# One more step of distance between scores, transpositions and products with V, in two attention loops of a transformer kernel

## Chip, cores and metric

The kernel runs on one core of a Trainium2 chip. The metric is the device time of one execution in microseconds (us); lower is better. The engines of the core are TensorE (PE in the profile, with PEld for its weight loads), VectorE (DVE), ScalarE (ACT), GpSimd (POOL) and SyncE (SP, which here only issues DMAs). Each engine takes its own instructions strictly in order and waits on semaphores of the others.

## The reference, cut to what matters

The reference is two blocks of two layers each. The first block is sparse attention with a short convolution, then latent attention, each followed by an MLP; the change doesn't touch it. The second block has a layer of differential attention and a layer of neighbourhood attention over 512 latent tokens and 256 context tokens, with 2048 inner features. Cut to its core:

```python
def diff_softmax_pair(q, k, v, lam, scale):          # 16 heads of two score maps each, V of width 128
    s = jnp.einsum('bqnd,bknd->bnqk', q, k) * scale
    p = jax.nn.softmax(s, axis=-1)                   # keys: 512 latent + 256 context
    w = p[:, :, 0] - lam * p[:, :, 1]
    return jnp.einsum('bhqk,bkhe->bqhe', w, v)
# then: rms_norm(o, subln_g) * (1 - lam_init) * silu(z) @ w_out

# neighbourhood attention, 32 heads of width 64, for one row of queries:
    s = einsum(q_row, k_band) * scale + bias          # masked outside the window
    p = softmax(concat([s, s_ctx]))
    o = einsum(p_band, v_band) + einsum(p_ctx, v_ctx)
# then: o * silu(z) @ w_out
```

Both layers begin with the projections q, k, v and z of their normalized input.

## The kernel before

All products are made in a split form: every operand x is kept as a high part and a low part (x minus the high part), and three matmuls stand for one (`mm3`, lines 578 to 580). The weights are split on the way in: `WeightStream.split` copies the high part on ACT (line 272) and subtracts on POOL (line 273). A ring of four split units is kept; `hold` releases the used ones, and each `tick` splits at most one more.

Both attention layers run through `second`. It plans a loop of steps by hand: `fill[i]` holds the "pieces" of step i (24 matmuls of a projection into one 128x256 tile of PSUM, named `mm`, some 2.85 us of PE), `early[i]` and `extra[i]` hold small work for ACT, DVE, POOL and the queues. The pieces of head group g + 1 (q, k, v) and of z of group g are made between the attention steps of group g, so PE always has matmuls to go on with. `defer` puts work off to the beginning of the next step.

**Differential attention** (`diff_run`): 8 groups g, 2 pairs p, 6 query tiles t, so 96 units and 12 steps to a group. The text counts steps inside a group from 0; step 12 is step 0 of the next group. In step i:

- A: scores of unit i into the PSUM tiles `s2` (2 buffers of 1024 columns), for the two maps. Tiles t = 0 to 3 have 768 keys ("wide"), t = 4 and 5 have the 256 context keys.
- B on DVE: the negated row maximum (L2051). E on ACT: the exponentials, with their row sums. `Dm` on DVE: the reciprocal (L2071), two scalings (L2072), the weighted difference (L2073, tile `X`) and EPS times the squared row sum (L2076, tile `oe`).
- T of unit i - 1: PE transposes the difference (L2088) into PSUM tiles `tp` (2 buffers; a wide unit takes two, a narrow one one); ACT and DVE copy it to `wt`.
- G of unit i - 2: the product with V (L2101), 12 matmuls in what the trace counts for a wide unit, 4 for a narrow one.
- `Hn` and `H2` follow a pair's last tile: norm of the output, then six transpositions into two `tp` tiles (L2128), scaled on DVE by z's gate (L2129), and a DMA to DRAM. H2 comes HD = 6 steps after the last tile's scores, at the end of steps 11 (pair 0) and 5 of the next group (pair 1).
- `stack` (L1778), in `extra`: transposes q or k of the next group into one `tp` tile and splits it; at the end of steps 6, 7, 8, 9, 11 (two of them), 12 and 13.

**Neighbourhood attention** (`na_run`): 8 groups, 4 heads, 4 query tiles, so 128 units and 16 steps to a group. A (L2212, L2213) makes 512 scores, B (L2221) adds bias and takes the maximum, E the exponentials, `Dm` reciprocal and scaling (L2231, L2232, tile `X`). T of unit i - 1 is four transpositions (L2239); ACT copies the high part `pth`, DVE makes the low part `ptl`. After the fourth tile of a head, G (L2249, L2254) multiplies with V, and `add` (L2261) on DVE joins the halves one step later. Steps 12 to 17 end with stacks of the next group; `dup` copies the upper half of KH and KL by a DMA on POOL's queue (L1802) after steps 14 and 17, and the scores of step 16 need the first of them. `tp` has 3 buffers here.

The order of a step on PE is A, the first piece (neighbourhood: its first half), T (neighbourhood: G, then T), the remaining pieces, G (differential), H2, stacks.

Of the kernel before, what the change touches and what calls it, by code (L numbers as in the profile page):

```python
# [12 lines left out]
F32 = mybir.dt.float32  # L13
# [215 lines left out]
Z7 = (3, 4, 5, 6, 7, 7)  # L229
Y7 = (7, 7, 7, 7, 8, 8, 8, 8)  # L230
O7 = [9, 10, 10, 11, 11, 12, 12, 13, 14, 15, 16, 17]
Z73 = (2, 2, 3, 4)
Y73 = (4, 4, 5, 5, 5, 6, 6, 6)
O73 = [7 + j for j in range(10)]
O1 = (59, 62, 64, 66)
# [138 lines left out]
class Net:  # L374
# [1240 lines left out]
    def second(s, L, nx):  # L1615
# [222 lines left out]
        for g in range(8):  # L1838
            t0 = ns * g
            zz = [z_piece(g, b, t) for b in range(2) for t in range(0, qw, 256)]  # L1840
            qk = [piece("q", g + 1, i) for i in range(nq)] + [piece("k", g + 1, i) for i in range(6)]
            if diff and g < 7:
                vv = [piece("v", g + 1, i) for i in range(6)]
                rest = zz + vv if g < 6 else zz[:3] + vv + zz[3:]
                for t, x in zip((6, 6, 7, 7, 8, 8, 9, 9, 10, 10, 11, 11) if g < 6 else (6, 7, 8, 8, 9, 10, 11, 12, 13, 13, 14, 15), rest):
                    put(fill, t0 + t, x)
                for j in range(6):
                    put(fill, t0 + j, *qk[2 * j:2 * j + 2])
                at = (6, 6, 7, 8, 8, 9, 9, 10, 11, 12, 13, 14) if g < 6 else (6, 7, 7, 8, 8, 9, 13, 13, 14, 14, 15, 15)
                gates_at([t0 + t for t in at], g, [(b, c) for b in range(2) for c in range(6)])  # L1850
                for t, f in zip((6, 7, 8, 9), stacks("q", 0) + stacks("k", 0)):
                    put(extra, t0 + t, f)
                put(extra, t0 + 9, lambda: dup(0))
                for t, f in zip((11, 11, 12, 13), stacks("q", 1) + stacks("k", 1)):
                    put(extra, t0 + t, f)
                put(extra, t0 + 13, lambda: dup(1))
            elif diff:
                for t, x in zip(Z7, zz):
                    put(fill, t0 + t, x)
                put(extra, t0 + 2, lambda: y_tile(), *[lambda b=b: y_dma(b) for b in range(5)])  # L1860
                gates_at([t0 + t for t in (4, 5, 6, 7, 8, 9, 10, 11, 12, 13, 14, 15)], g, [(b, c) for b in range(2) for c in range(6)])
                put(extra, t0 + 5, lambda: y_dma(5))
                for b in range(8):
                    put(early, t0 + Y7[b], lambda b=b: y_split(b))
            else:
                if g < 7:
                    vv = [piece("v", g + 1, i) for i in range(6)]
                    for t, x in zip((0, 1, 2, 3, 4, 5, 6, 7, 8, 9, 10, 11, 12, 13) + ((13, 14, 14, 15, 15, 16) if g < 6 else (14, 15, 15, 16, 16, 17)), qk + zz + vv):
                        put(fill, t0 + t, x)
                    gates_at([t0 + t for t in (12, 13, 13, 14, 14, 15, 15, 16)], g, [(b, c) for b in range(2) for c in range(4)])  # L1870
                    for t, f in zip((12, 13, 14), stacks("q", 0) + stacks("k", 0)):
                        put(extra, t0 + t, f)
                    put(extra, t0 + 14, lambda: dup(0))
                    for t, f in zip((15, 16, 17), stacks("q", 1) + stacks("k", 1)):
                        put(extra, t0 + t, f)
                    put(extra, t0 + 17, lambda: dup(1))
                    put(extra, t0 + 18, lambda g=g: v_stash(g + 1))
                else:
                    for t, x in zip(Z73, zz):
                        put(fill, t0 + t, x)  # L1880
                    gates_at([t0 + t for t in (7, 8, 9, 10, 11, 12, 13, 14)], g, [(b, c) for b in range(2) for c in range(4)])
                    put(extra, t0 + 2, *[lambda b=b: y_dma(b) for b in range(6)])
                    for b in range(8):
                        put(extra, t0 + Y73[b], lambda b=b: y_split(b))
            if g == 7:
                for j, (c, i) in enumerate([(c, i) for c in range(nq) for i in range(nq)][:12 if diff else 10]):
                    acc[c, i] = st[:, j]
                    put(fill, t0 + (O7 if diff else O73)[j], o_piece(c, i))
# [123 lines left out]
    def diff_run(s, c):  # L2012
# [3 lines left out]
        wt = s.pool("wt", 2)  # L2016
        ob = s.pool("ob", 2)
        units = [(g, p, t) for g in range(8) for p in range(2) for t in range(6)]
        d, O = {}, {}
        ei = [0]  # L2020

        def A(u):
# [31 lines left out]
        def E(u):  # L2054
            g, p, t = u
            x = d[u]
            for j in range(2):
                h = 4 * t + 2 * p + j
                S = x["s"][j]
                e = X[ei[0] % 4][:, :S.shape[-1]]  # L2060
                ei[0] += 1
                sm = s.sml.tile([128, 1], F32, name=f"df_s{j}")
                s.act(e, S, AF.Exp, bias=x["nb"][j], scale=-1.0, acc=sm)
                x["e"].append((e, sm))

        def Dm(u):
            g, p, t = u
            x = d[u]
            (ea, sa), (eb, sb) = x["e"]
            rb = s.sml.tile([128, 1], F32, name="df_rb")  # L2070
            nc.vector.reciprocal(rb, sb)  # L2071
            nc.vector.scalar_tensor_tensor(rb, sa, nlam, rb, OP.mult, OP.mult)  # L2072
            nc.vector.scalar_tensor_tensor(ea, eb, rb, ea, OP.mult, OP.add)  # L2073
            if t == 0:
                O[g, p] = ob.tile([128, 6, 128], F32, name="ob"), ob.tile([128, 6], F32, name="oss"), ob.tile([128, 6], F32, name="oe")
            nc.vector.scalar_tensor_tensor(O[g, p][2][:, t:t + 1], sa, EPS, sa, OP.mult, OP.mult)  # L2076

        def T(u):
            g, p, t = u
# [14 lines left out]
        def G(u):  # L2094
            g, p, t = u
            x = d.pop(u)
            nk = 6 if t < 4 else 2
            ps = s.mm.tile([128, 512], F32, name="mm")[:, :128]
            for k in range(nk):
                kb = k if t < 4 else 4 + k  # L2100
                nc.tensor.matmul(ps, x["w"][:, k], V[g][:, kb, p * 128:(p + 1) * 128], start=k == 0, stop=k == nk - 1)  # L2101
            o, ss, _ = O[g, p]
            s.act(o[:, t], ps, AF.Copy)
            sq = ob.tile([128, 128], F32, name="df_sq")
            s.act(sq, ps, AF.Square, acc=ss[:, t:t + 1])

        def Hn(g, p):
            o, ss, oe = O[g, p]
            v, y, a = [s.sml.tile([128, 6], F32, name=f"df_{k}") for k in "vya"]
            nc.vector.scalar_tensor_tensor(v, ss, 1.0 / 128, oe, OP.mult, OP.add)  # L2110
            s.act(y, v, AF.Ln)
            s.act(y, y, AF.Exp, scale=-0.5)

            def two():
                nc.vector.tensor_tensor(a, y, y, OP.mult)
                nc.vector.tensor_tensor(a, a, v, OP.mult)
                nc.vector.tensor_scalar(a, a, -0.5, 1.5, OP.mult, OP.add)
                nc.vector.tensor_tensor(y, y, a, OP.mult)
                nc.gpsimd.tensor_tensor(o, o, y.unsqueeze(2).to_broadcast([128, 6, 128]), OP.mult)

            s.defer(two)
# [8 lines left out]
            nc.sync.dma_start(yd[2 * g + p], o.rearrange("p a b -> p (a b)"))  # L2130

        N = len(units)
        HD = 6
        for i in range(N + HD + 1):
            u = [units[i - k] if 0 <= i - k < N else None for k in range(HD + 1)]
            pcs = c.fill.get(i, [])
# [4 lines left out]
                s.whole(mm)  # L2141
            if u[0]:
                B(u[0])
            if u[1]:
                T(u[1])
            for _, ev in pcs[:1]:
                ev()
            if u[0]:
# [2 lines left out]
                s.whole(mm)  # L2151
            for f in c.early.get(i, []):
                f()
            if u[2]:
                G(u[2])
            if u[0]:
                Dm(u[0])
            for _, ev in pcs[1:]:
                ev()
            if u[3] and u[3][2] == 5:  # L2160
                Hn(*u[3][:2])
            if u[HD] and u[HD][2] == 5:
                H2(*u[HD][:2])
            for f in c.extra.get(i, []):
# [2 lines left out]
    def na_run(s, c):  # L2167
# [11 lines left out]
            nc.vector.memset(t[64:128, 0, 128:256], NEG)  # L2179
        pth, ptl = [gp.tile([128, 4, 4, 128], F32R, name=n) for n in ("pth", "ptl")]  # L2180
        rpb = X[0][:, 640:896]
        P = [X[0][:, :512], X[1][:, :512]]
        tmp = X[2][:, 0:512]
        ofs = [X[2][:, 512:1024], X[3][:, 0:512]]
        d = {}
# [29 lines left out]
        def B(u, i):  # L2215
# [3 lines left out]
            t = bm[h % 2]  # L2219
            x["nb"], x["sm"] = [s.sml.tile([128, 1], F32, name=f"na_{k}") for k in ("nb", "s")]  # L2220
            nc.vector.tensor_tensor_reduce(S, S, t[:, 1:3] if j else t[:, 0:3:2], -1.0, 3e38, OP.add, OP.min, x["nb"])  # L2221
            x["P"] = P[i % 2]

        def E(u):
            x = d[u]
# [43 lines left out]
        units = [(g, h, j) for g in range(8) for h in range(4) for j in range(4)]  # L2269
        N = len(units)  # L2270
        bias(0)
        for i in range(N + 3):
            u = [units[i - k] if 0 <= i - k < N else None for k in range(3)]
            pcs = c.fill.get(i, [])
            if u[0]:
                A(u[0])
# [3 lines left out]
            next(p1, None)  # L2280
            if u[0]:
                B(u[0], i)
            if u[2] and u[2][2] == 3:
                G(*u[2][:2])
            if u[1]:
                T(u[1])
            if u[0]:
                E(u[0])
            for _ in p1:
# [9 lines left out]
                Dm(u[0])  # L2299
            for _, ev in pcs[1:]:  # L2300
                ev()
            if r == 3 and 0 < g < 7:
                Y(g - 1, 0)
                Y(g - 1, 1)
            if r == 1 and g == 7 or r == 15 and g == 7:
                Y(g - (r == 1), 0)
            if r == 2 and g > 6:
                Y(g - 1, 1)
            for f in c.extra.get(i, []):
                f()  # L2310
# [15 lines left out]
```

## Time and profile before

| what | us |
|---|---|
| median of three runs | 3223.96 (3220.66 to 3226.64) |
| the profiled execution, its own time | 3223.14 |
| its span, first to last instruction | 3221.3 |
| PE busy | 3067.4 (95%) |
| differential attention loop, in the trace | 1447 to 2296 |
| neighbourhood attention loop | 2470 to 3154 |

The span is what one execution took between its first and last instruction; 1.8 us lie around it. A busy PE is the time in which a matmul is under way. In a wait list each row is one engine's idle time in front of a line, with what ended it, the total in us, the number of times and the longest. In a timeline row the idle time before an instruction stands in brackets.

### The profile page before, as it was taken

To read this page: it belongs to the slowest core of one execution; us is meant where nothing else is said; L and a number is where in the kernel's file an instruction comes from. 1 tells how busy PE (TensorE), PEld (TensorE's weight loads), DVE (VectorE), ACT (ScalarE), POOL (GpSimd) and SP (SyncE) were. 2 spreads that over 40 slices of the span, in tenths; PEclk is the share of its full clock that TensorE was granted. 3 is DMA by queue.
4 is the path that set the end of the run, shared out by engine and by line. 5 is a ranking of instruction groups with operands and counts; after the bars stand their busy time and mean duration, and the time that the engine had idled before them with its cause. 6 is when DMAs were issued, how large, how long until landed. Compare 5 with 4: busy or idle time off the path is not lost.

```text
span 3221.3 us, 58548 instructions
## 1 busy us (share of the span) xinstructions
PE 3067.4 (95%) x22868; PEld 2882.8 (89%) x22868; DVE 2132.6 (66%) x4241; ACT 1605.0 (50%) x3795; POOL 1473.9 (46%) x1296
## 2 busy tenths in 40 slices
PE   7999999998889999999999999998999999999989
PEld 7888889887788898789999999998999999999988
DVE  4886444556874344656777877788455777777864
ACT  4544533335665333455555555555325555555552
POOL 4432344443333444465544654462355444444444
PEclk9999999999999999999999999999999999999999
DMA  3122333433123344331221222123323322323334
GB/s 122 60 73 73 106 129 126 150 95 99 37 65 107 125 144 136 111 94 52 63 65 60 62 63 65 60 62 95 116 98 97 84 81 75 88 80 89 88 91 138
DMA packets 96128, 291.93 MB, mean 91 GB/s; under 512 B 19166, under 2 KB 28638, under 8 KB 92780
## 3 DMA queue, kind: packets, MB, share of 16 engines
q1 hardware_dynamic: 89148, 259.01, 24.8%
q0 software_dynamic: 5120, 25.17, 3.6%
q10 hardware_dynamic: 1584, 4.00, 0.4%
q8 instruction: 181, 2.97, 0.4%
q14 instruction: 95, 0.78, 0.1%
HBM read 244.05 MB, written 18.92 MB: 82 GB/s over the span
## 4 chain that ended last, share of the span: by engine, by line
PE 49%; DVE 13%; ACT 4%; issue 4%; DMA 3%; POOL 2%; SPq 0%; POOLq 0%; DVEq 0%; ACTq 0%
PE mm L578 13%; PE mm L580 12%; PE mm L579 12%; PE mm L2101 3%; DMA KL<-KL 1%; POOL w_lo L273 1%; PE tp L2239 1%; ACT X L406 1%; PE tp L2088 1%; DVE s L2051 1%; PE mm L2254 1%; PE mm L2249 1%; DVE X L2232 1%; PE s L2040 1%; DVE ge L1765 1%
## 5 line engine op out<-in xcount | busy, mean ns | idle before, releaser
L273 POOL TENSOR_TENSOR w_lo<-w_raw,w_hi 128x1024 fp32r<-128x1024 f32 (+2 forms) x350 | 879.0, 2517 | 1019.7 <-ACT w_hi L272 994.5
L578 PE MATMUL mm<-w_hi,hh 128*128 128x256 f32 (+3 forms) x2880 | 840.0, 292 | 7.9 <-ACT df_sq L406 2.6
L579 PE MATMUL mm<-w_lo,hh 128*128 128x256 f32 (+3 forms) x2880 | 820.3, 285 | 11.3 <-POOL w_lo L273 11.3
L580 PE MATMUL mm<-w_hi,hl 128*128 128x256 f32 (+3 forms) x2880 | 821.3, 285 | 3.3 <-POOL hl L409 3.0
L578 PEld LDWEIGHTS mm<-w_hi,hh 128*128 128x128 f32 x2880 | 550.5, 191 | 19.3 <-ACT df_sq L406 8.5
L579 PEld LDWEIGHTS mm<-w_lo,hh 128*128 128x128 f32 x2880 | 551.2, 191 | 18.4 <-POOL w_lo L273 13.8
L580 PEld LDWEIGHTS mm<-w_hi,hl 128*128 128x128 f32 x2880 | 549.6, 191 | 6.4 <-POOL hl L409 5.5
L272 ACT CAST w_hi<-w_raw 128x1024 fp32r<-128x1024 f32 (+2 forms) x355 | 366.1, 1035 | 206.0 <-PE mm L580 171.3
L578 PE MATMUL mm<-hh,w_hi 128*128 128x256 f32 (+1 forms) x1408 | 455.3, 323 | 3.0 <-DVE M L1083 2.8
L579 PE MATMUL mm<-hl,w_hi 128*128 128x256 f32 (+1 forms) x1408 | 448.3, 318 | 0.6
L580 PE MATMUL mm<-hh,w_lo 128*128 128x256 f32 (+1 forms) x1408 | 446.8, 317 | 1.2 <-DVE w_lo L273 1.2
L578 PEld LDWEIGHTS mm<-hh,w_hi 128*128 128x128 f32 x1408 | 265.9, 189 | 30.9 <-issue 5.2
L579 PE MATMUL mm<-w_lo,gh 128*128 128x256 f32 x1024 | 287.1, 280 | 1.4 <-POOL w_lo L273 1.4
L578 PE MATMUL mm<-w_hi,gh 128*128 128x256 f32 x1024 | 287.6, 281 | 0.0
L580 PE MATMUL mm<-w_hi,gl 128*128 128x256 f32 x1024 | 287.1, 280 | 0.1
L579 PEld LDWEIGHTS mm<-hl,w_hi 128*128 128x128 f32 x1408 | 265.9, 189 | 22.3 <-DVE hl L340 1.7
L580 PEld LDWEIGHTS mm<-hh,w_lo 128*128 128x128 f32 x1408 | 265.6, 189 | 21.9 <-DVE w_lo L273 1.6
L1262 DVE SCALAR_TENSOR_TENSOR macc<-modw,cg,macc 128x1024 f32<-128x1024 f32 x84 | 201.6, 2444 | 29.0 <-DMA modw<-in_mod 29.0
L579 PEld LDWEIGHTS mm<-w_lo,gh 128*128 128x128 f32 x1024 | 193.0, 188 | 1.9 <-POOL w_lo L273 1.6
L578 PEld LDWEIGHTS mm<-w_hi,gh 128*128 128x128 f32 x1024 | 193.3, 189 | 0.4
L580 PEld LDWEIGHTS mm<-w_hi,gl 128*128 128x128 f32 x1024 | 193.0, 189 | 0.5 <-DVE gl L409 0.5
L409 DVE TENSOR_TENSOR gl<-rsq,gh 128x512 fp32r<-128x512 f32 x64 | 45.6, 713 | 220.4 <-ACT gh L406 220.4
(373 smaller groups left out, 6880.4 us busy)
## 6 DMA issues: line engine op xcount, KB each, us to landing
w_raw<-in_w SPq DMA_DIRECT2D x336, 512.0 KB, 3.5
modw<-in_mod SPq DMA_DIRECT2D x24, 1024.0 KB, 5.8
KH<-KH POOLq DMA_DIRECT2D x32, 384.0 KB, 4.0
KL<-KL POOLq DMA_DIRECT2D x32, 384.0 KB, 5.1
xs<-X SPq DMA_DIRECT2D x12, 512.0 KB, 3.1
X<-xs SPq DMA_DIRECT2D x12, 512.0 KB, 6.7
yd<-ob SPq DMA_DIRECT2D x16, 384.0 KB, 2.3
w_raw<-in_w SPq DMA_DIRECT2D x8, 552.0 KB, 4.7
```

What stands on the lines that cost most here:

```text
L272: nc.scalar.copy(hi[:, :m], raw[:, :m])
L273: (eng or nc.gpsimd).tensor_tensor(lo[:, :m], raw[:, :m], hi.bitcast(F32)[:, :m], OP.subtract)
L406: return s.nc.scalar.activation(out, in_, func, bias=bias, scale=scale, **kw)
L409: (eng or s.nc.vector).tensor_tensor(lo, x, hi.bitcast(F32), OP.subtract)
L578: mm(ps, ah, bh, start=first, stop=False)
L579: mm(ps, ah, bl, start=False, stop=False)
L580: mm(ps, al, bh, start=False, stop=last)
L1262: nc.vector.scalar_tensor_tensor(acc[:, v], w[:, k2], cv, acc[:, v], OP.mult, OP.add)
L1765: nc.vector.reciprocal(x, x)
L2040: nc.tensor.matmul(o, q, KH[:, h, a:b], start=True, stop=False)
L2051: nc.vector.tensor_tensor_reduce(S, S, s.zero.to_broadcast(list(S.shape)), nrq[:, h:h + 1], 3e38, OP.add, OP.min, nb)
L2101: nc.tensor.matmul(ps, x["w"][:, k], V[g][:, kb, p * 128:(p + 1) * 128], start=k == 0, stop=k == nk - 1)
```

## The change

Transpositions take the unit of two steps before (T(u[2])) and the products with V that of three steps before (G(u[3])), in both loops. What follows later moves by one step: `Hn`, `H2` (HD = 7), Y and its DMAs, and some of the plan in `second`. More buffers hold what lives longer: three instead of two for the differences `ea` in turn (the second map always takes X[3]), a third tile P2 in the neighbourhood loop, three buffers for `oe`, which is now a tile of its own.

```diff
-Z73 = (2, 2, 3, 4)
+Z73 = (2, 3, 4, 4)
...
-                put(extra, t0 + 5, lambda: y_dma(5))
+                put(extra, t0 + 6, lambda: y_dma(5))
...
-                    for t, x in zip((0, ..., 13) + ((13, 14, 14, 15, 15, 16) if g < 6 else (14, 15, 15, 16, 16, 17)), qk + zz + vv):
+                    for t, x in zip((0, ..., 13) + ((14, 14, 15, 15, 16, 16) if g < 6 else (14, 15, 15, 16, 16, 17)), qk + zz + vv):
...
-                e = X[ei[0] % 4][:, :S.shape[-1]]
-                ei[0] += 1
+                e = X[3 if j else ei[0] % 3][:, :S.shape[-1]]
+                ei[0] += 1 - j
...
-                O[g, p] = ob.tile([128, 6, 128], F32, name="ob"), ob.tile([128, 6], F32, name="oss"), ob.tile([128, 6], F32, name="oe")
-            nc.vector.scalar_tensor_tensor(O[g, p][2][:, t:t + 1], sa, EPS, sa, OP.mult, OP.mult)
+                oe[g, p] = ob.tile([128, 6], F32, name="oe", bufs=3)
+            nc.vector.scalar_tensor_tensor(oe[g, p][:, t:t + 1], sa, EPS, sa, OP.mult, OP.mult)
...
-        HD = 6
+        HD = 7
...
-            if u[1]:
-                T(u[1])
+            if u[2]:
+                T(u[2])
...
-            if u[2]:
-                G(u[2])
+            if u[3]:
+                G(u[3])
...
-            if u[3] and u[3][2] == 5:
-                Hn(*u[3][:2])
+            if u[4] and u[4][2] == 5:
+                Hn(*u[4][:2])
...
-        P = [X[0][:, :512], X[1][:, :512]]
+        P = [X[0][:, :512], X[1][:, :512], gp.tile([128, 512], F32, name="P2")]
...
-            x["P"] = P[i % 2]
+            x["P"] = P[i % 3]
...
-            if u[2] and u[2][2] == 3:
-                G(*u[2][:2])
-            if u[1]:
-                T(u[1])
+            if u[3] and u[3][2] == 3:
+                G(*u[3][:2])
+            if u[2]:
+                T(u[2])
...
-            if r == 3 and 0 < g < 7:
+            if r == 4 and 0 < g < 7:
...
-            if r == 2 and g > 6:
+            if r == 3 and g > 6:
```

In the neighbourhood loop the six pieces of v move: step 13 has one piece instead of two, step 16 has three (the two last of v and the first of the next q) instead of two. G moves from steps 1, 5, 9, 13 of a group to steps 2, 6, 10, 14, `add` with it.

## Rows read from the trace of the kernel before

**Rows 1.** The page's head: the span.
```profile
span 3221.3 us, 58548 instructions
```

**Rows 2.** Both loops as windows: length, busy per engine, granted clock, DMA.
```profile
core 0: us, PE busy (x) PEld busy (x) DVE busy (x) ACT busy (x) POOL busy (x), PEclk, DMA share, GB/s
1447.00:2296.00 849.00, 819.82 (x6612) 793.27 (x6613) 636.98 (x1394) 464.02 (x1367) 427.21 (x497) 0.99 0.22 64
2470.00:3154.00 684.00, 649.10 (x5060) 627.28 (x5059) 529.66 (x1100) 389.14 (x930) 309.27 (x305) 0.98 0.30 84
```

**Rows 3.** PE's waits in the differential loop.
```profile
PE tp L2088 <- DVE oe L2076: 5.4, 2, 4.9
PE tp L1778 <- DVE ob L2129: 5.2, 7, 1.4
PE tp L2088 <- DVE KL L409: 3.8, 8, 1.9
```

**Rows 4.** PE's waits in the neighbourhood loop.
```profile
PE tp L2239 <- DVE X L2232: 27.5, 22, 3.5
PE s L2213 <- DMA KL<-KL: 5.5, 8, 1.4
```

**Rows 5.** Timeline, differential loop, end of a step 6 and start of 7.
```profile
1720.33 0.61 PE L2101 MATMUL mm<-VS,wt 128*128 128x128 f32 x4
...
1720.78 0.60 PE L1778 MATMUL tp<-ident,st 128*128 128x128 f32 x4
1721.12 2.76 POOL L273 TENSOR_TENSOR w_lo<-w_raw,w_hi 128x1024 fp32r<-128x1024 f32 x1 [2.22 <-ACT w_hi L272]
1721.53 2.36 DVE L2076 SCALAR_TENSOR_TENSOR oe<-df_s 128x1 f32<-128x1 f32 x1
```

**Rows 6.** Timeline, differential loop, end of a step 11.
```profile
1764.24 1.50 PE L2101 MATMUL mm<-VS,wt 128*128 128x128 f32 x12
...
1765.58 0.82 PE L2128 MATMUL tp<-ident,ob 128*128 128x128 f32 x6
...
1766.22 1.14 DVE L2129 SCALAR_TENSOR_TENSOR ob<-tp,gs,SZ 128x512 f32<-128x512 f32 x2 [1.94 <-PE tp L2128]
1767.02 0.88 PE L1778 MATMUL tp<-ident,st 128*128 128x128 f32 x6 [0.62 <-DVE ob L2129]
```

**Rows 7.** Timeline, differential loop, end of the step 12 after it.
```profile
1775.49 0.60 PE L1778 MATMUL tp<-ident,st 128*128 128x128 f32 x4
...
1776.60 2.39 DVE L2076 SCALAR_TENSOR_TENSOR oe<-df_s 128x1 f32<-128x1 f32 x1
```

**Rows 8.** Timeline, neighbourhood loop: the copy of KL's lower half, steps 15 and 16.
```profile
2627.89 1.00 DVE L1791 SCALAR_TENSOR_TENSOR KL<-tp,par,KH 64x256 fp32r<-64x256 f32 x2 [0.52 <-ACT KH L406]
...
2634.76 0.39 PE L2213 MATMUL s<-KL,QS 128*128 128x256 f32 x1 [1.27 <-DMA KL<-KL]
```

**Rows 9.** Timeline, neighbourhood loop, step 18 (step 2 of the next group).
```profile
2648.84 2.62 DVE L2232 TENSOR_SCALAR X<-X,na_r 128x512 f32<-128x512 f32 x1
2651.49 0.75 DVE L2261 TENSOR_TENSOR X<-mm,X 64x448 f32<-64x448 f32 x2
...
2651.61 0.63 PE L2239 MATMUL tp<-ident,X 128*128 128x128 f32 x4 [1.95 <-DVE X L2232]
```

**Rows 10.** Timeline of PE: single long waits, from step 14 of group 6 on.
```profile
3054.77 0.63 PE L2239 MATMUL tp<-ident,X 128*128 128x128 f32 x4 [2.98 <-DVE X L2232]
...
3098.87 1.11 PE L2239 MATMUL tp<-ident,X 128*128 128x128 f32 x4 [3.50 <-DVE X L2232]
3127.82 1.00 PE L2239 MATMUL tp<-ident,X 128*128 128x128 f32 x4 [1.86 <-DVE X L2232]
3148.63 1.09 PE L2239 MATMUL tp<-ident,X 128*128 128x128 f32 x4 [2.36 <-DVE X L2232]
```

**Rows 11.** Windows behind the waits at 3054.77 and 3098.87 (columns as in rows 2).
```profile
3055.00:3059.00 4.00, 4.00 (x36) 4.00 (x35) 3.87 (x9) 1.71 (x5) 1.84 (x4) 1.00 0.95 247
3099.00:3103.00 4.00, 4.00 (x17) 3.69 (x17) 3.39 (x9) 2.52 (x7) 1.55 (x2) 0.50 0.41 125
```

More of the change, by code (lines that the diff above doesn't have):

```diff
@@ L1867, in second @@
                     vv = [piece("v", g + 1, i) for i in range(6)]
-                    for t, x in zip((0, 1, 2, 3, 4, 5, 6, 7, 8, 9, 10, 11, 12, 13) + ((13, 14, 14, 15, 15, 16) if g < 6 else (14, 15, 15, 16, 16, 17)), qk + zz + vv):
+                    for t, x in zip((0, 1, 2, 3, 4, 5, 6, 7, 8, 9, 10, 11, 12, 13) + ((14, 14, 15, 15, 16, 16) if g < 6 else (14, 15, 15, 16, 16, 17)), qk + zz + vv):
                         put(fill, t0 + t, x)
@@ L2018, in diff_run @@
         units = [(g, p, t) for g in range(8) for p in range(2) for t in range(6)]
-        d, O = {}, {}
+        d, O, oe = {}, {}, {}
         ei = [0]
@@ L2101, in G @@
                 nc.tensor.matmul(ps, x["w"][:, k], V[g][:, kb, p * 128:(p + 1) * 128], start=k == 0, stop=k == nk - 1)
-            o, ss, _ = O[g, p]
+            if t == 0:
+                O[g, p] = ob.tile([128, 6, 128], F32, name="ob"), ob.tile([128, 6], F32, name="oss")
+            o, ss = O[g, p]
             s.act(o[:, t], ps, AF.Copy)
@@ L2107, in Hn @@
         def Hn(g, p):
-            o, ss, oe = O[g, p]
+            o, ss = O[g, p]
             v, y, a = [s.sml.tile([128, 6], F32, name=f"df_{k}") for k in "vya"]
-            nc.vector.scalar_tensor_tensor(v, ss, 1.0 / 128, oe, OP.mult, OP.add)
+            nc.vector.scalar_tensor_tensor(v, ss, 1.0 / 128, oe.pop((g, p)), OP.mult, OP.add)
             s.act(y, v, AF.Ln)
@@ L2271, in na_run @@
         bias(0)
-        for i in range(N + 3):
-            u = [units[i - k] if 0 <= i - k < N else None for k in range(3)]
+        for i in range(N + 4):
+            u = [units[i - k] if 0 <= i - k < N else None for k in range(4)]
             pcs = c.fill.get(i, [])
```

## Prediction

> **What bounds the kernel now.** I read the page's head first: one execution spans 3221.3 us [rows 1], and its own time is 3223.14, so 1.84 lie around the span. The sum below is made against 3223.1, 0.8 under the median of the runs. The windows of the two loops come next [rows 2]. The reader is to see that PE bounds both: it is busy 819.82 of 849 us in the differential loop and 649.10 of 684 in the neighbourhood loop, at a granted clock of 0.99 and 0.98, while DVE has 637 and 530. The number of matmuls stays the same, so the change can only act on PE's idle time, 29.2 us and 34.9 us. Of this the lists of PE's waits say how much belongs to the transpositions. In the neighbourhood loop T waits 27.5 us, in 22 places, for the scaling of the unit just before [rows 4]. In the differential loop T waits for `Dm` 5.4 us, 4.9 of them at one place in the drain [rows 3]; its 3.8 us behind KL's copy are a wait for a `tp` buffer, which more distance to the scores doesn't touch. So the neighbourhood part has something to win, and the differential part little. The timelines tell what comes next.
>
> **Neighbourhood loop.** In step 18, T stands 1.95 us because DVE's scaling of the unit before takes 2.62 us there [rows 9]. With T one step later, that scaling has a step of some 4.5 us more. Sixteen waits of this kind in the steady steps sum to 16.5 us (27.5 less five of the end and the turn, 11.0). The next limits are the scores, which need E of two steps before, G, which needs the low part of T one step earlier, and the three `tp` buffers; each keeps most of a step of slack. I take the whole: -16.5.
>
> The other five singly. The 2.98 at 3054.77 [rows 10] is given back a step later, where the scores wait for the KL copy in any case: 0. The 3.50 at 3098.87, with 1.1 us of small waits around it, stands behind the chain of `y_split`, and that chain begins earlier when the Y DMA isn't queued on SP behind one that waits for POOL; bounds 0 and -4.6, I take -2.0. The 1.86 at 3127.82 goes: -1.9. The last, 2.36 at 3148.63, is at the end, where T still waits for a `Dm` of the last units: -1.3, bounds 0 and -2.4.
>
> What is late next is the copy of KL. The low half is written by DVE in step 15, a DMA on POOL's queue copies it, and the scores of step 16 wait for that DMA, 1.27 us in the place shown [rows 8], 5.5 us in 8 waits in all [rows 4]. G, and with it `add`, moves to steps 2, 6, 10, 14. Thus two `add` instructions, 0.75 us together [rows 9], now stand on DVE ahead of KL's copy, where 0.52 us of idle time covers part [rows 8]; T's low part in that step moves as well. Growth for each of six groups: 0.25 from these two rows, up to 2 if the stretched scaling of 2.62 falls ahead of it (2.62 less its unstretched half microsecond). I take 0.6, nearer the low row: +3.6. The pieces of v that move between steps 13 and 16 keep their sum.
>
> Sum: -16.5 - 2.0 - 1.9 - 1.3 + 3.6 = **-18.1**.
>
> **Differential loop.** T and G give back little; what matters is `H2`, which moves from step 11 to 12 and from step 5 to 6 of the next group. In step 11 today: six transpositions begin at 1765.58, the first half of the scaling frees the first `tp` buffer 0.80 after its start at 1766.22, and the stack begins at 1767.02 [rows 6]. It begins 1.44 after H2; G's twelve matmuls show 1.34 us from start to start, 0.11 each, so six cost 0.67 and the loss is 0.77.
>
> In steps 6 and 12 three things differ. First, the unit whose `Dm` runs there is a wide one, and its last instruction, `oe` on 128x1 elements, takes 2.36 and 2.39 us [rows 5, 7]: it begins at 1721.53, 0.41 after POOL's split of weights (1721.12, 2.76 long), and ends with it at 1723.89. Second, a stack follows there too, and needs H2's first `tp` buffer; DVE frees it only after `oe`. Third, G is a wide unit's, so twelve matmuls instead of four: 0.89 later by the rows (1.34 less 0.45).
>
> Step 6: the stack comes to PE at 1720.78 + 0.89 + 0.67 = 1722.34, and the buffer is free at 1721.53 + 2.36 + 0.80 = 1724.69: a wait of 2.35, five times: +11.8. A sixth one, in group 6, lies where DVE is the fuller engine; bounds 0 and 2.45, I take +1.7. Step 12: 1775.49 + 0.89 + 0.67 = 1777.05 against 1776.60 + 2.39 + 0.80 = 1779.79: 2.74, six times: +16.5; the seventh takes the place of the 1.4 of today [rows 3]: 0. Behind the waiting stack in PE's order stand the next scores and all pieces, so the wait is PE's own loss.
>
> Removed: step 11's 0.77, six times, -4.6. T in step 13 is now a narrow one and needs no second buffer: of the 3.8 behind KL's copy six small ones go, -1.7. In the drain the 4.9 [rows 3] goes, but the scores of the same steps wait for the exponentials fed by the same chain; bounds 0 and -5.4, I take -2.5. The new tiles and the counters of `ea` issue no instruction. The one more step of drain in each loop costs nothing, since pieces of the output projection still run over it.
>
> Sum: 11.8 + 1.7 + 16.5 - 4.6 - 1.7 - 2.5 = **+21.2**.
>
> On the stretched `oe`: a row of 128x1 that takes 2.36 us ends within 0.01 us of POOL's subtraction [rows 5]. The Trainium skill, "SBUF — State Buffer", section "Who interferes with whom", says that a DVE instruction with two SBUF inputs contends with a GpSimd instruction that reads SBUF, and that whoever issues first keeps the shared ports for its whole instruction. This case's trace agrees, and the rule speaks against the change, for it puts H2's scaling behind the blocked instruction. By it the order of issue decides: were `oe` first, it would take about its bare time, and the sum would be the one of rival A.
>
> **Together:** +21.2 - 18.1 = +3.1, so 3223.1 + 3.1 = 3226.2. By 0.2%, 6.4 us, about what a measurement of this kernel can tell from no change, this is no change: a gain in one loop and a loss in the other.
>
> **The rivals.**
>
> *A, faster: the collision of H2 with `oe` doesn't come about.* POOL begins only 0.41 us before `oe` [rows 5]; G is longer, T's copies lie elsewhere, and a split that comes over 0.41 later finds `oe` done. Then the stack waits behind H2 as in step 11: twelve times 0.77, less 4.6, 1.7 and 2.5, is +0.4. With -18.1: 3205.4. Against it: ACT, which releases POOL, does the exponentials before and is little moved, and rows 5 and 7, of two different steps, show the same pattern. Chance 0.20.
>
> *B, slower: the copy of KL gives back the neighbourhood's gain.* The waits of today show that this DMA has no slack [rows 8]. With x us per group the total is 3.1 - 3.6 + 6x, slower by 0.2% from x = 1.2 on. With 2 us, the other bound, 3234.6. Against it: the pieces in front of the scores stay as many. Chance 0.17.
>
> *C, slower: the granted clock falls behind the new waits.* After the wait of 3.50 at 3098.87 the window shows a granted clock of 0.50, the level of 1.2 GHz, for 4 us [rows 11]: 2 us of work lost beside the wait itself. After the wait of 2.98 at 3054.77, in dense work, it shows 1.00, the level of 2.4 GHz [rows 11]. The twelve new waits of 2.4 to 2.7 lie in dense work, as the second. Two falls decide (3.1 + 4 is over 6.4); twelve would give 3226.2 + 24 = 3250. Chance 0.12.
>
> *D, the same mechanism with its unknown terms at their low ends:* KL not later (-3.6), group 6 without its wait (-1.7), the drain's whole 5.4 won (-2.9): 3.1 - 8.2 = -5.1, so 3218. Chance 0.10.
>
> **How the numbers follow.** The forecast, with its terms a few us off either way (3220 to 3233), has 0.41 and gives 3226. The range goes from 3202, A with three us more won at the end of the neighbourhood loop, to 3241, B's bound with one us more in each of six groups; outside lie most of C and a little of A, under 0.2 together. Faster by over 0.2% (under 3217): A and half of D, 0.25. Within: six in seven of the forecast, half of D, a little of B, 0.42. Slower: B, C and the rest of the forecast, 0.33.
>
> **What would show it.** In the changed kernel's wait lists, the stacks (L1778) behind `ob` should rise from 5.2 to over 30 us, with some twelve waits of 2.3 to 2.8 at the ends of steps 6 and 12, and `oe` still 2.4 long in front of them. T (L2239) behind `X` should fall from 27.5 to some 5, and the DMA of KL rise from 5.5 to about 9. The differential loop should last some 21 us longer and the neighbourhood loop some 18 less. The prediction is wrong if `oe` is short in steps 6 and 12 (A), if the scores' waits for KL pass 12 us (B), if windows behind the new waits show 0.50 (C), or if T still waits for something one step later: its `tp` buffers or the copies of `wt`, which I take to have a step's slack.

## The result and the profile after

The changed kernel takes 3242.92 us in the median of five runs (3239.65 to 3254.62) against 3223.96 before (also of five): a ratio of 1.0070 (1.0048 to 1.0092), 19 us or some 0.6% slower by the medians. The profiled execution is one of the longer ones, 3251.59 us with a span of 3249.8. The five times go with the mean granted clock of the execution: 0.987 gives 3239.65, 0.986 gives 3242.88 and 3242.92, 0.983 gives 3251.59 and 3254.62. So the comparison below is made by stages, and the clock is kept apart.

I cut both executions at the first scores of each loop and at the last matmul of G. The stage of the differential loop, with what follows it up to the next loop, went from 1447.1 to 2470.4 and lasted 1023.3 us; it now lasts 1057.5. The neighbourhood loop went from 2470.4 to 3153.7 and lasted 683.3; it now lasts 673.4. Ahead of the loops, where nothing was changed, 4.1 us more passed; that start lies between 1445.7 and 1452.0 in the profiles of this study. The tail is the same. The two stages as windows, of the changed kernel:

```profile
core 0: us, PE busy (x) PEld busy (x) DVE busy (x) ACT busy (x) POOL busy (x), PEclk, DMA share, GB/s
1451.20:2508.70 1057.50, 1001.56 (x8029) 976.37 (x8029) 729.71 (x1553) 525.56 (x1488) 513.05 (x583) 0.98 0.24 71
2508.70:3182.10 673.40, 644.73 (x5053) 624.37 (x5052) 524.39 (x1100) 390.46 (x930) 304.69 (x304) 0.98 0.30 85
```

and the same two stages of the kernel before:

```profile
1447.10:2470.40 1023.30, 989.35 (x8028) 961.82 (x8029) 723.27 (x1554) 527.32 (x1489) 516.84 (x583) 0.99 0.25 74
2470.40:3153.70 683.30, 648.40 (x5054) 626.58 (x5053) 529.66 (x1100) 389.14 (x930) 308.89 (x304) 0.98 0.30 84
```

The number of PE's matmuls in the records is the same to one. In the differential stage PE's idle time rose by 22.0, to 55.9 us, and its busy time, for the same matmuls, by 12.2 us; the granted clock is 0.98 there instead of 0.99. In the neighbourhood loop idle time fell from 34.9 to 28.7; the other 3.7 of the 9.9 us lie in busy time, at the same granted clock, and no run here explains them. The lists of waits of the changed kernel, first the differential stage, then the other, say what it consists of:

```profile
PE tp L1778 <- DVE ob L2131: 32.4, 13, 2.8
PE s L2040 <- ACT X L406: 10.0, 4, 5.0
...
PE tp L2088 <- ACT wt L406: 1.9, 1, 1.9
```

```profile
PE mm L578 <- DVE X L2263: 16.6, 7, 2.4
PE mm L580 <- POOL hl L409: 3.7, 1, 3.7
PE s L2214 <- DMA KH<-KH: 3.4, 1, 3.4
PE mm L2251 <- DVE ptl L409: 2.3, 8, 0.5
PE mm L2251 <- ACT pth L406: 1.4, 2, 0.7
PE s L2215 <- DMA KL<-KL: 1.3, 2, 0.7
```

The stacks (L1778) wait 32.4 us for H2's scaling, where they waited 5.2 [rows 3]. In the neighbourhood loop T no longer waits for its scaling at all, where it waited 27.5 [rows 4]; but a piece (L578) now waits 16.6 for `add` (L2263), and G (L2251) 3.7 for the copies of the transposed tile. The end of a step 12 in the timeline of the changed kernel, to be held against [rows 6, 7]:

```profile
1562.64 1.50 PE L2101 MATMUL mm<-VS,wt 128*128 128x128 f32 x12
...
1563.60 1.02 DVE L2073 SCALAR_TENSOR_TENSOR X<-X,df_rb,X 128x768 f32<-128x768 f32 x1
1563.67 3.15 POOL L273 TENSOR_TENSOR w_lo<-w_raw,w_hi 128x1024 fp32r<-128x1024 f32 x1
1563.97 0.82 PE L2130 MATMUL tp<-ident,ob 128*128 128x128 f32 x6
1564.54 2.30 DVE L2076 SCALAR_TENSOR_TENSOR oe<-df_s 128x1 f32<-128x1 f32 x1
...
1566.76 1.13 DVE L2131 SCALAR_TENSOR_TENSOR ob<-tp,gs,SZ 128x512 f32<-128x512 f32 x2
...
1567.55 0.66 PE L1778 MATMUL tp<-ident,st 128*128 128x128 f32 x4 [2.76 <-DVE ob L2131]
```

`oe`, on 128x1 elements, begins at 1564.54 and ends with POOL's split at 1566.8; only then comes H2's scaling, and 0.79 later the stack. Eleven of the thirteen waits look like this, with an `oe` of 2.30 to 2.35 us ahead of them. The last two, in group 6, don't. There DVE waits for the exponentials, the whole of `Dm` comes late, and `oe` is short:

```profile
2180.49 0.16 DVE L2071 RECIPROCAL df_rb<-df_s 128x1 f32<-128x1 f32 x1 [3.22 <-ACT X L406]
...
2181.88 0.15 DVE L2076 SCALAR_TENSOR_TENSOR oe<-df_s 128x1 f32<-128x1 f32 x1
...
2182.75 0.66 PE L1778 MATMUL tp<-ident,st 128*128 128x128 f32 x4 [2.75 <-DVE ob L2131]
```

The windows of 4 us behind three of the thirteen waits (2.76, 2.05 and 2.03 us long):

```profile
1568.00:1572.00 4.00, 4.00 (x21) 3.78 (x20) 3.02 (x7) 1.19 (x2) 1.50 (x3) 0.63 0.59 218
1624.00:1628.00 4.00, 4.00 (x20) 3.61 (x19) 2.59 (x5) 1.19 (x2) 3.47 (x6) 0.62 0.57 217
1737.00:1741.00 4.00, 4.00 (x31) 3.83 (x32) 2.82 (x7) 1.19 (x2) 3.14 (x6) 1.00 0.68 229
```

The granted clock falls to 0.63 and 0.62 over the window, with 21 and 20 matmuls instead of 31; behind the third wait it stays at 1.00. It fell behind 8 of the 13 waits in this execution. In two others that were profiled with the same differential code (the runs e1 and e5 below) it fell behind 7 and 5 of the same 13. In what follows the "half-rate loss" of a stage is the sum of (1 - granted clock) x 4 us over its windows of 4 us below 0.97: 6.8 us in the differential stage before, 25.4 after; each of the eight falls makes 1.6 to 1.7 of it.

In the neighbourhood loop, the timeline of the changed kernel at the end of a step 14 and in step 15:

```profile
2574.23 2.36 POOL L273 TENSOR_TENSOR w_lo<-w_raw,w_hi 128x1024 fp32r<-128x1024 f32 x1 [2.61 <-ACT w_hi L272]
...
2575.19 1.68 DVE L2234 TENSOR_SCALAR P<-P,na_r 128x512 f32<-128x512 f32 x1
...
2576.79 0.74 DVE L2263 TENSOR_TENSOR X<-mm,X 64x448 f32<-64x448 f32 x2
...
2577.68 0.36 PE L578 MATMUL mm<-w_hi,hh 128*128 128x256 f32 x1 [2.41 <-DVE X L2263]
```

A scaling that begins while POOL's split runs again takes 1.68 us instead of 0.49, and ends 0.28 behind the split. T has a step more and doesn't wait for it; but `add`, which now comes in step 15, stands behind it on DVE and frees one of the three `mm` buffers, and the piece that needs that buffer waits 2.41 us.

### The profile page after: what moved, and what is told of

Its sections match the earlier page's. It is cut to its first block, busy times and chain, and to the rows that moved or that the text cites. A ratio compares the mean times of both kernels' runs of the same rounds, so it can differ in the third digit from the quotient of the medians.

```text
span 3249.8 us, 58458 instructions
## 1 busy us (share of the span) xinstructions
PE 3078.2 (95%) x22868; PEld 2897.2 (89%) x22868; DVE 2132.6 (66%) x4241; ACT 1604.9 (49%) x3795; POOL 1466.5 (45%) x1296
## 5 line engine op out<-in xcount | busy, mean ns | idle before, releaser
L578 PE MATMUL mm<-w_hi,hh 128*128 128x256 f32 (+3 forms) x2880 | 844.0, 293 | 24.0 <-DVE X L2263 16.6
L579 PE MATMUL mm<-w_lo,hh 128*128 128x256 f32 (+3 forms) x2880 | 823.4, 286 | 12.2 <-POOL w_lo L273 10.7
L578 PEld LDWEIGHTS mm<-w_hi,hh 128*128 128x128 f32 x2880 | 554.8, 193 | 37.2 <-issue 19.2
L578 PE MATMUL mm<-hh,w_hi 128*128 128x256 f32 (+1 forms) x1408 | 456.1, 324 | 3.0 <-DVE M L1083 2.9
L578 PEld LDWEIGHTS mm<-hh,w_hi 128*128 128x128 f32 x1408 | 267.0, 190 | 30.9 <-issue 5.2
L578 PE MATMUL mm<-w_hi,gh 128*128 128x256 f32 x1024 | 287.6, 281 | 0.0
L578 PEld LDWEIGHTS mm<-w_hi,gh 128*128 128x128 f32 x1024 | 193.2, 189 | 0.4
```

Of the source, the lines that this page charges most:

```text
L578: mm(ps, ah, bh, start=first, stop=False)
L579: mm(ps, ah, bl, start=False, stop=False)
```

## The experiments

All twelve ran in three groups of four, each beside the kernel before on the same chip; the three groups had three chips, on which the kernel before gave 3223.26, 3224.50 and 3225.64. Between groups a ratio therefore says more than a median. The ratios are to the kernel before; the stages and the half-rate loss (hr) are those of one profiled execution, in us.

| run | median us | ratio (interval) | differential stage, hr | neighbourhood loop, hr |
|---|---|---|---|---|
| before | 3223.96 | | 1023.3, 6.8 | 683.3, 13.6 |
| changed | 3242.92 | 1.0070 (1.0048 to 1.0092) | 1057.5, 25.4 | 673.4, 13.6 |
| e1_diff_part | 3250.06 | 1.0085 (1.0071 to 1.0099) | 1055.1, 22.1 | 676.7, 6.8 |
| e2_neighbour_part | 3218.68 | 0.9984 (0.9975 to 0.9993) | 1025.1, 8.6 | 673.9, 13.6 |
| e3_h2_back | 3213.83 | 0.9970 (0.9959 to 0.9981) | 1021.2, 12.0 | 673.4, 13.6 |
| e4_oe_first | 3216.45 | 0.9981 (0.9972 to 0.9990) | 1026.3, 12.0 | 671.5, 11.9 |
| e5_add_early | 3240.20 | 1.0048 (1.0036 to 1.0060) | 1054.1, 20.4 | 663.4, 5.1 |
| e6_fill_wait | 3256.93 | 1.0101 (1.0088 to 1.0114) | 1067.5, 6.8 | 668.9, 8.4 |
| e7_h2_back_add | 3204.07 | 0.9935 (0.9923 to 0.9947) | 1019.1, 10.0 | 666.9, 8.5 |
| e8_h2_back_oe_add | 3201.06 | 0.9930 (0.9918 to 0.9942) | 1015.8, 8.6 | 664.3, 6.9 |
| e9_fill_half | 3237.18 | 1.0039 (1.0026 to 1.0051) | 1046.3, 8.5 | 676.1, 17.0 |
| e10_stacks_early | 3204.88 | 0.9944 (0.9930 to 0.9958) | 1016.8, 8.6 | 670.6, 11.9 |
| e11_h2_5 | 3186.09 | 0.9879 (0.9865 to 0.9892) | 1007.0, 10.1 | 664.7, 5.2 |
| e12_stacks_early_h2_5 | 3199.35 | 0.9916 (0.9903 to 0.9930) | 1009.2, 13.6 | 671.4, 11.9 |

**Each loop alone** (the other loop's lines as before).

> The change in the differential loop alone; the neighbourhood loop as before. Theory 1 (H2 stands behind a stretched oe in steps 6 and 12, and the granted clock falls behind the waits): 32 us of waits of L1778 behind ob in 13 waits, 21 us net, and 10 to 18 us more by the clock, so 3224 + 31 to 39, less a few us of other waits that go: 3245 to 3262. Rival 2 (the loss is one of both loops together, or of the program as a whole): the time lies less than 10 us above 3224.

> The change in the neighbourhood loop alone; the differential loop as before. Theory 1: T's waits of 27.5 us go, the waits of the pieces for add (L2263 in the whole change, 16.6 us in 7) and a few others come: 10 us under before, 3214 (3209 to 3219). Rival 2 (the distance itself costs, in either loop): 3224 or more.

The differential part alone costs 0.85%, with 32.7 us of the stacks' waits in 13; the neighbourhood part alone gains 0.16%. Theory 1 holds for the place, rival 2 falls. The gain of the second is about half of what the neighbourhood stages of the two first profiles suggest: e1's neighbourhood loop, the code of before, lasts 676.7 against 683.3, with 6.8 less half-rate loss. Idle time says it better: 34.9 and 33.0 with the old code, 28.7 and 28.9 with the new.

**H2 where it was.**

```diff
-        HD = 7
+        HD = 6
```

> The whole change, but H2 again 6 steps after the last tile's scores, at the end of steps 11 and 5. Theory 1: the stacks' waits behind ob fall from 32.4 us to 5 or 6, the half-rate stretches behind them vanish, and the time is 3203 to 3215. Rival 3 (three steps to the products with V make the loss, by the tp and mm buffers or by later norms): the waits come back under other names, and the time stays above 3230.

The waits for `ob` are 5.5 us again, in 7, the stage is 36.3 us shorter than with the change, and the whole is 0.30% faster than before. Rival 3 falls: the distance of T and G costs nothing in sum. (The scores' wait for the exponentials is 10.3 us here too, against 4.2 before, but T's wait for `oe`, 5.4, is gone.)

**`oe` ahead of X.**

```diff
+            nc.vector.scalar_tensor_tensor(oe[g, p][:, t:t + 1], sa, EPS, sa, OP.mult, OP.mult)
             nc.vector.scalar_tensor_tensor(ea, eb, rb, ea, OP.mult, OP.add)
-            nc.vector.scalar_tensor_tensor(oe[g, p][:, t:t + 1], sa, EPS, sa, OP.mult, OP.mult)
```

> The whole change, but in Dm the small instruction oe is issued on DVE before the weighted difference X, no longer after it; H2 stays at steps 12 and 6. Theory 1 (the two-input instruction on DVE that begins after POOL's split has to wait for it; X begins before the split): oe takes some 0.1 us, H2's scaling follows X directly, the stacks wait 0.3 to 0.9 us each, 4 to 11 us in 13 waits instead of 32.4, and the time is 3205 to 3220. Rival 4 (POOL's split delays whatever stands on DVE there, whichever began first): X is stretched to over 2 us, the waits stay near 2.5 each, and the time stays above 3235.

The timeline of this run at the end of its step 12, DVE and POOL, and the stack on PE:

```profile
1558.97 0.15 DVE L2075 SCALAR_TENSOR_TENSOR oe<-df_s 128x1 f32<-128x1 f32 x1
1559.09 1.02 DVE L2076 SCALAR_TENSOR_TENSOR X<-X,df_rb,X 128x768 f32<-128x768 f32 x1
1559.16 3.18 POOL L273 TENSOR_TENSOR w_lo<-w_raw,w_hi 128x1024 fp32r<-128x1024 f32 x1
...
1560.10 1.14 DVE L2131 SCALAR_TENSOR_TENSOR ob<-tp,gs,SZ 128x512 f32<-128x512 f32 x2
1560.90 0.66 PE L1778 MATMUL tp<-ident,st 128*128 128x128 f32 x4 [0.63 <-DVE ob L2131]
```

`oe` takes 0.15 instead of 2.30, and X keeps its 1.02. It is the split that takes longer where X begins ahead of it: 3.18 here and 3.15 in the changed kernel, against 2.36 at 2574.23, where the split began first. The waits are 0.62 to 0.69 in eleven places; the last two stay at 2.7, since no stretched `oe` made them. In sum they are 12.5, a little over the 4 to 11 expected. Two instructions in the other order take back 26 us of the medians; rival 4 falls. The Trainium skill, "SBUF — State Buffer", section "Who interferes with whom", has the first to issue keep the shared ports: X begins 0.07 before POOL here and is not stretched, `oe` behind POOL was. It also says that a DVE instruction with no more than one SBUF input, outside the two-port modes, doesn't contend: H2's scaling, which takes one input from PSUM, runs its 1.14 in the middle of POOL's split.

**Matmuls in place of the wait.** Behind each H2 up to step 84:

```diff
                 H2(*u[HD][:2])
+                if i < 85:
+                    junk = s.mm.tile([128, 512], F32, name="mm")[:, :128]
+                    v = V[u[0][0]][:, 0, 0:128]
+                    for k in range(20):
+                        nc.tensor.matmul(junk, v, v, start=k == 0, stop=k == 19)
```

> The whole change, and after each H2 up to step 84 PE gets 20 more matmuls of 128 columns into a tile that nobody reads (added work; the computation is the same), some 2.2 us, in the place where it waits for ob. The waits themselves stay as long. Theory 1 with rival C of the prediction (the granted clock falls because PE stands still there): the waits of L1778 fall from 32.4 us to under 10, the half-rate stretches in the differential loop go, and the time falls by 8 to 18 us, to 3225 to 3235. Rival 6 (the falls of the clock have another cause, or cost nothing of the time): the time stays at 3240 or above.

> As e6_fill_wait, but with 10 more matmuls behind each H2 instead of 20. In that run 20 of them ran as 40 passes and took 4.73 us, longer than the wait; 10 should take some 2.4, about as long as the wait. Theory 1 with rival C: PE's waits for ob fall from 32.4 us to under 5 while its added work is 13 times 2.4, 31 us, so the waiting time itself stays; what is won is the clock alone: 25.4 us lost by the granted clock in the differential stage fall to some 7, and the time falls by 10 to 18 us from the changed kernel's 3243, to 3225 to 3233. Rival 6 (the falls of the clock cost nothing of the time): 3240 or above.

The first missed: 20 matmuls ran as 40 passes in 4.73 us, longer than the wait, and the time rose to 3257. Yet the half-rate loss is down to 6.8. The stage adds up: eleven times 4.73 and, in group 6, twice 4.63 are 61.3 of work more; with 32.4 of waits less the stage would be 28.9 longer. It is 10.0 longer, so 18.9 came back, and the half-rate loss fell by 18.6. With half as many, the timeline of PE at the end of its step 12, and the window of 4 us behind it:

```profile
1564.09 2.50 PE L2170 MATMUL mm<-VS 128*128 128x128 f32 x20
...
1566.91 0.66 PE L1778 MATMUL tp<-ident,st 128*128 128x128 f32 x4 [0.32 <-DVE ob L2131]
```

```profile
1567.00:1571.00 4.00, 4.00 (x31) 3.83 (x32) 3.01 (x6) 1.19 (x2) 1.87 (x4) 1.00 0.68 229
```

Eleven times 2.50 and twice 2.40 are 32.3 of useless work; 29.4 of waits are gone, and the stage is 11.2 shorter: 14.1 came back for 16.9 less half-rate loss. The median, 3237, lies between the two expectations. It is 6 us under the changed kernel's, by the ratios 10, where 10 to 18 were forecast. The stack still begins 0.79 behind the start of H2's scaling; only what follows runs at the full clock. In neither run did the clock fall behind any of the 13 places. So these falls come of PE standing still, and they cost time.

**`add` in G's own step.** `G` returns `add`, and the step issues it ahead of `Dm`:

```diff
-            s.defer(add)
+            return add
...
+            if add:
+                add()
             if u[0]:
                 Dm(u[0])
```

> The whole change, but in the neighbourhood loop add is issued on DVE at the end of G's own step, before that step's scaling, and no longer at the start of the next step. Theory 1 (a piece waits for a buffer of mm that add frees, and add stands behind a scaling stretched by POOL's split): the 16.6 us of waits of the pieces go, the half-rate stretches behind them too, and the time falls by 14 to 26 us from the changed kernel's 3243, to 3217 to 3229. Rival 5 (PE only runs into the next limit: the mm buffers are held as long by other readers, or add, now ahead of the scaling, delays the next transpositions as much): the waits come back under another name and the time stays above 3236.

The 16.6 us are gone, the neighbourhood loop is 10.0 shorter, half-rate loss 5.1 instead of 13.6. But the copies are late now. From the list of waits of that loop:

```profile
PE s L2214 <- DMA KH<-KH: 6.4, 4, 4.2
PE s L2215 <- DMA KL<-KL: 6.0, 8, 1.2
```

12.4 us against the changed kernel's 4.7: of the 16.6 that went, 8 came back at the next limit. The time, 3240, missed the 3217 to 3229 expected: it is under the changed kernel's by 3 in the medians and by 7 in the ratios, and the two intervals overlap. In the time rival 5 is right. The profiled loop itself is 10.0 shorter, and e7 gained 9.8 on e3 by their medians, in the same group.

**Both cures.**

> H2 again 6 steps behind (as in the run e3_h2_back) and add at the end of G's step, the rest of the change as it is. Theory 1: both causes are gone, 14 to 26 us under that run's 3213.8: 3188 to 3200. Rival 5: above 3207.

> As e7_h2_back_add, and oe issued before X in Dm. Theory 1: in steps 11 and 5 H2 stands behind no stretched oe, so the order changes little there: within 4 us of e7_h2_back_add. Rival 4 (any instruction behind POOL's split is late, wherever H2 stands): over 5 us faster than it.

e7 gains those 9.8 us on e3, less than the 14 to 26 that were forecast, with the copies' 11.5 us of waits as in e5. e8 is 3 us faster than e7, as theory 1 has it, within what these runs can tell.

**The copies a step earlier, and H2 where no stack follows** (both on top of e8).

```diff
-                    for t, f in zip((12, 13, 14), stacks("q", 0) + stacks("k", 0)):
+                    for t, f in zip((11, 12, 13), stacks("q", 0) + stacks("k", 0)):
-                    put(extra, t0 + 14, lambda: dup(0))
+                    put(extra, t0 + 13, lambda: dup(0))
...
-        HD = 6
+        HD = 5
```

> As e8_h2_back_oe_add, and in the neighbourhood loop the stacks of pair 0 and the copies of KH and KL one step earlier (steps 11, 12, 13; copies after 13). Theory 1 (with the waits for add gone, the scores of step 16 wait for these copies, 7.5 us for KL and 5.1 for KH, as the prediction's rival B has it): both waits fall under 2 us and the time by 6 to 14 us, to 3187 to 3195. Rival 7 (the stack, a step earlier, collides with k's norm or with the scaling of another step): the waits come back at the stacks, and the time stays within 4 us of 3201.

> As e8_h2_back_oe_add, but H2 5 steps behind, at the end of steps 10 and 4, where no stack follows. Theory 1 (a stack behind H2 needs the tp buffer that DVE's scaling frees): the 5.4 us of L1778 behind ob in 7 waits go, 3 to 7 us faster than that run's 3201. Rival 8 (the norm, in POOL's queue behind the split of weights, is now too late for H2's transpositions): waits of a microsecond or more in front of them, and the time is over 3205.

> e10_stacks_early and e11_h2_5 in one. Theory 1: the two gains add up, 9 to 20 us under 3201: 3181 to 3192.

e10 stays 4 us above e8 instead of 6 to 14 below. The earlier stacks take the copies' waits away and put others in their place: G waits for its low part, in e10's list

```profile
PE mm L2251 <- DVE ptl L409: 14.9, 15, 1.8
...
PE mm L2251 <- ACT pth L406: 6.1, 9, 0.7
```

because KL's copy on DVE now stands in front of that low part in the step in which G needs it: at 2524.29 in e10 it begins, 1.51 long, and G's next matmul waits until 2527.19. Rival 7 holds for the time, at another place than it named, and e12 pays for it again: 13 us above e11 instead of below. H2 at the ends of steps 10 and 4 needs no such trade: no wait for `ob` is left in e11, and its stage is 8.8 shorter than e8's. e11 is the best version, 3186.09 us, 1.21% faster than before. That is 15.0 under e8, where 3 to 7 were forecast for 5.4 us of waits: the stage gives 8.8, 5.0 lie ahead of the loops, where the two kernels are the same, and the rest is small.

## Why the prediction was wrong

The range, 3202 to 3241, ended 2 us below the median, and the sign was right only as a bare +0.1%. Step by step:

- **The collision in steps 6 and 12: right, to its size.** Forecast: five waits of 2.35, one of 1.7, six of 2.74, and one in place of the old one. Measured: 13, of 2.75 to 2.83 at step 12 and 2.03 to 2.07 at step 6, with 2.75 in group 6. e4 shows the cause of eleven: `oe` behind POOL's split. The two of group 6 come of the late `Dm` and stay in e4. `ob` costs 27.2 more, where the sum had 25.4 with the 4.6 of step 11 taken off.
- **The rest of the differential sum: near by luck.** The stage's idle time rose by 22.0 where the sum had 21.2, but single terms missed. The drain cost some 2 us instead of giving back 2.5: T's 5.4 went, the scores' waits for the exponentials rose from 4.2 to 10.0, and T waits 1.9 for a copy of `wt`, which the prediction had taken to have a step's slack. T's waits for the copy of QS, which the prediction didn't speak of, went instead (2.9 to 0.3).
- **Rival C, at 0.12: this step failed.** "The twelve new waits of 2.4 to 2.7 lie in dense work, as the second", and so keep the clock. They didn't: it fell behind 8 of 13. One wait of 2.98 without a fall [rows 10, 11] was taken as the rule for all. The trace of the kernel before spoke against it: six steady waits of T of 1.95 to 1.98 us, in dense work, and the clock fell behind three. Windows of the kernel before (columns as above) behind two of them, at 2651.61 [rows 9] and at 2822.80:

```profile
2652.00:2656.00 4.00, 3.55 (x29) 3.25 (x26) 3.58 (x10) 1.93 (x5) 2.33 (x5) 1.00 1.01 229
2823.00:2827.00 4.00, 4.00 (x23) 3.81 (x22) 3.59 (x10) 1.92 (x5) 2.33 (x4) 0.64 0.95 240
```

  The price per fall was about right, 1.7 us measured against 2. The half-rate loss of the stage rose by 18.6, of which the eight falls make 13.5 (the rest lies at the stage's start, in the drain and at its end); PE's busy time rose by 12.2. e6 and e9 show that these falls come with the standing still.
- **Neighbourhood loop: "each keeps most of a step of slack. I take the whole: -16.5" failed.** The list of next limits left out the `mm` buffers. `add` holds one, and it stands behind the stretched scaling on DVE, as [rows 9] already showed; I priced its 0.75 us ahead of KL's copy, and asked neither what stands ahead of it nor who waits for it. So six waits of about 2.4 and one of 1.99 replaced T's. G's wait for the copies of the tile, to which the prediction gave a step of slack, costs another 3.7. PE's idle time fell by 6.2 instead of 18.1. e5 shows the cause of the larger part. (The steady waits were seventeen, not sixteen; their sum holds.)
- **KL's copy:** forecast to be 0.6 later in each group. In the changed kernel it seemed to vanish (1.3 us left), because the wait for `add` comes a step earlier and covers it; with that wait gone it is there (e5: 6.0 for KL, 6.4 for KH). At the end, the wait for KH's copy in group 6 (3.4) takes the place of the 2.98, which is the +0 of the prediction. The wait for POOL's part of `y_split` (`hl`, 3.7) is new; the prediction took 2.0 off the 3.50 that stood behind that chain.
- **Rival A** didn't come about by itself, since POOL kept its place; e4 made it happen. e4 less the changed kernel is -26 where the prediction's A lay 21 under its forecast.
- **What it adds up to.** The two profiled executions differ by 28.5 us where the sum had 3.1. Of the 25.4 between, 12.2 are the half-rate matmuls of the differential stage, 8.2 the neighbourhood stage, 4.1 lie ahead of the loops, and 0.8 is the differential idle time. The profiled execution has a mean granted clock of 0.983, the median one 0.986; the forecast of 3226 lies 17 us under the median.

## What to carry to other kernels

When a consumer moves a step away from its producer, list every ring on the way, the buffers that its readers free too, and look for the slowest instruction that stands ahead of that release on the same engine. A moved instruction is priced by its new neighbours in the queue: here two small instructions in the other order, or one epilogue placed where no user of the same buffers follows, were worth more than the change. A wait of PE in dense work should be priced at itself and a chance of another 1.7 us of half-rate matmuls. In three executions of the differential loop the clock fell behind 3 of 15 waits of 2.03 to 2.13 us (step 6), and behind 17 of 24 waits of 2.75 to 2.84 (step 12 and group 6).

## What the runs showed of the hardware that was not expected

- The same wait in the same program drops the granted clock in one group and not in the next, and in one execution and not in another (8, 7 and 5 of the same 13 waits in the changed kernel, e1 and e5): in the changed kernel, behind 2.05 us at 1623.39 it fell, behind 2.03 at 1736.92 it did not; of the waits for `add`, all near 2.4 us, the windows behind 2577.68 and 2661.94 show 1.00, those behind 2746.05 and 2831.77 show 0.58.
- A neighbourhood loop of the same code lasted 683.3 and 676.7 us in two executions (before and e1), with 13.6 and 6.8 us of half-rate loss.
- `add`, which takes one input from PSUM, is not held up by POOL's split (0.68 in e5, begun 0.82 after the split); the scaling of 128x512 in SBUF is (1.68 in the changed kernel and 2.62 before, against 0.49).
